# A hybrid mixer trunk: low weight parts behind high ones, additions moved off GpSimd, a new order of the first projections

## The chip, the cores and the metric

One core of a Trainium2 chip runs the whole program. The metric is device time in microseconds, from one launch; lower is better. Times before and after are medians of runs on a chip. TensorE, VectorE, ScalarE and GpSimd each execute their own list of instructions in order and wait for one another through semaphores; SyncE (SP) issues the DMAs.

## The reference

512 latent tokens and 256 context tokens of width 1024 go through two layers. In each layer all tokens are normalised, modulated and multiplied by one wide input matrix; three branches (gated DeltaNet, RG-LRU, neighbourhood attention) work on parts of the result; their outputs are gated, projected, merged and multiplied by an output matrix. The second layer yields latents alone.

```
h_lat = rms_norm(x, g_pre) * (1 + scale_l) + shift_l        # the same for context
p = h @ w_in        # split: DeltaNet q,k,v / gates / RG-LRU in / attention q,k,v / merge gates
q, k, v = silu(conv4(p[0]));  q, k = l2_normalize(q), l2_normalize(k)
q, k = axial_rope(q), axial_rope(k)                         # latents only
# DeltaNet, per chunk and direction, 4 heads:
u = w_v - w_k @ S;  o = (q*exp(gc)) @ S + (q k^T * decay) @ u
S = S * g_tail + (k * exp(gc[-1] - gc))^T @ u               # "key tail" times u
# merge
merged = sum_b sigmoid(gate_b) * (y_b @ w_branch[b]);  y = merged @ w_out
x = x + gate_l * rms_norm(y, g_post)
```

## The kernel before

**Arithmetic.** A float32 product is made of float16 matmuls: each weight block is split into a high part (`whi`, ScalarE) and a low part (`wlo`, VectorE: raw minus high), and the hidden state `h` likewise into two parts. `seg()` multiplies, for each of 8 (or 4) blocks of the contraction, high by high, high by low and low by high into one PSUM bank, 512 latent columns and then 256 context columns.

**Order by a planner.** The program's instruction lists are written by a planner, `Flow`. Python generators (tasks) issue instructions; `note()` assigns each VectorE, ScalarE and GpSimd instruction an estimated duration, and a task that yields a number sleeps that long in planned time. `fl.until(tile)` is the planned time until a tile is ready; `fl.fetched()` plans when a load lands. Tasks that are due run by rank; `main()` has the last rank, 9, and issues all projections, so a task with work ready puts its matmuls ahead of main()'s. A yield is no instruction and no wait on the chip: it only moves what other tasks issue meanwhile. `copy()` picks VectorE or ScalarE by which is planned to be sooner.

**Weights.** `schedule()` lists a layer's projections; `Weights` loads their blocks in that order through a ring of three raw buffers, splits them (`split()`; for attention and merge-gate weights, the names in `FINE`, in two parts of 4 blocks, each high part followed by its low part) and hands them out (`take()`).

**Around the layer.** `startup()` loads, normalises and modulates the tokens and computes the list's first three projections; at the end of a layer `layer()` does so for the next one, from `out_tail()`'s tiles. `out_tail()` takes one tile of 128 tokens through the output norm, the residual addition (first half of the columns on GpSimd, second on VectorE), the next layer's norm, eight transposes, the modulation (multiply on VectorE, addition on GpSimd) and the split into `h`.

**DeltaNet.** `gdn_front()` takes a projected tile (`a`) into a convolution buffer, of which there are two, shared with rotated queries; main() stands there until one is free. `gdn_prep()` convolves, transposes, rotates (products on VectorE, their sum on GpSimd) and normalises; one tile's preparation begins when the tile before has been read. `gdn_direction()` has one pass per direction over six chunks: `pre()` builds decay, key products (`lh`, `ll`) and the key tail `ktl` (GpSimd), `inverse()` the triangular inverse, `chain()` the recurrence.

**Modulation of the next layer.** `mod_rows()` is a side generator of main(): main() advances it with `next(side)` between merge-gate projections; it issues one load ahead and then four matmuls on the load before. It yields nothing that the planner reads.

Every VectorE, ScalarE and GpSimd instruction is recorded under line 195 (the `Engine` wrapper), matmuls under 258, transposes under 262, modulation matmuls under 467, so tiles' names tell them apart: `pl` are transposes in `gdn_prep`, `qt` and `kt` rotated queries and keys, `py` the output product, `xTp` the boundary's transposes, `pm` the modulation's product, `hx` the modulated tile, `lss` the squared norms, `pr` attention weights, `ld` a mask product of `lh`.

Of the kernel before, what the change touches and what calls it, by code (L numbers as in the profile page):

```python
# [17 lines left out]
P = 128  # L18
# [8 lines left out]
EPS = 1e-6  # L27
# [22 lines left out]
class Flow:  # L50
# [4 lines left out]
    def __init__(self):  # L55
        self.now, self.tasks = 0.0, []
        self.free, self.ready, self.used, self.near = {}, {}, {}, {}
        self.banks, self.kept, self.wire, self.ring = [None] * 5, set(), 0.0, []
        self.spent, self.touch, self.sp = set(), {}, 0.0
# [30 lines left out]
    def note(self, eng, op, args, kw):  # L90
        aps = [x for x in list(args) + list(kw.values()) if isinstance(x, bass.AP)]
        ins = aps[1:]
        n = max(math.prod(x.shape[1:]) for x in aps)
        start = max([self.free.get(eng, 0.0)] + [self.ready.get(x.name, 0.0)
                                                  - (LAT / 2 if self.near.get(x.name) == eng else 0.0) for x in ins])
        for x in ins:
            if x.space == PSUM and self.touch.get(x.name, (eng,))[0] != eng:
                start = max(start, self.touch[x.name][1] + LAT)
        if eng == "act":
            us = (n / 1200.0 + 0.09 + 0.09 * sum(isinstance(kw.get(x), bass.AP) for x in ("scale", "bias"))  # L100
                  + 0.2 * (kw.get("accum_out") is not None))
        elif op == "tensor_tensor_scan":
            us = n / 480.0 + 0.11
        elif eng == "pool":
            us = (n / 510.0 + 0.1 if n < 512 else n / 375.0) if op == "tensor_tensor" else n / 1000.0 + 0.12
        else:
            fast = (op == "tensor_scalar" and all(x.space == aps[0].space for x in ins)
                    or all(x.dtype == F16 for x in aps))
            us = n / (1920.0 if fast else 960.0) + 0.07 + 0.06 * sum(x.shape[1:] == (1,) for x in ins)
        end = self.free[eng] = start + us  # L110
        self.last = (start, us)
        for x in ins:
            self.used[x.name] = max(self.used.get(x.name, 0.0), end)
            if x.space == PSUM:
                self.touch[x.name] = (eng, end)
        for x in (aps[0], kw.get("accum_out")):
            if x is not None:
                self.ready[x.name] = end + LAT
                self.near[x.name] = eng
# [84 lines left out]
def schedule(l):  # L204
# [6 lines left out]
    s = [a0[0], a0[1], z[0], a0[2], z[1], a0[3], z[2], a0[4], z[3], a0[5]]  # L211
    s += kqv[0] + kqv[1] + kqv[2]
# [17 lines left out]
def build(tc, A, out):  # L230
# [88 lines left out]

    def rsqrt(dst, v, n, tag):  # L320
# [3 lines left out]
        V.tensor_scalar(yg[:, 0].bitcast(I32), v.bitcast(I32), -0.5, float(0x5F3759DF - (1 << 31)),  # L324
                        op0=OP.mult, op1=OP.add)
# [29 lines left out]
    class Weights:  # L355
# [19 lines left out]
        def split(self, pool_=None):  # L375
            if self.raw:
# [14 lines left out]
                for k in range(0, nk, step):  # L391
                    ks = slice(k, min(nk, k + step))
                    S.activation(hi[:, ks], raw[:, ks], AF.Copy, scale=SW)
                    yield fl.until(hi)
                    V.scalar_tensor_tensor(lo[:, ks], raw[:, ks], SW, hi[:, ks], op0=OP.mult, op1=OP.subtract)
# [3 lines left out]
        def take(self, key):  # L399
            yield lambda: self.pair and self.pair[0][3]  # L400
            hi, lo, k, _ = self.pair.pop(0)
            assert k == key, (k, key)
            return hi, lo
# [17 lines left out]
    def seg(dst, off, w, ks, nk, xs, a, b, ahead=False):  # L421

        hi, lo = w
        for k in ks:
            for n, (wt, part) in enumerate(((hi, 0), (hi, 1), (lo, 0))):
                mm(dst[:, a - off:b - off], wt[:, k, :], xs(part, k, a, b), start=(k == 0 and n == 0),
                   stop=(k == nk - 1 and n == 2))
                if n < 2:
                    yield 0.0
            if ahead and k == 0:  # L430
                W.ahead()
            yield 0.0
# [24 lines left out]
    def mod_rows(l, part, fin, load):  # L457
# [3 lines left out]
        yield  # L461
        pm = pst(f"pm{l}_{part}", [P, 512], keep=True)
        for k in range(KD):
# [8 lines left out]
            if k < KD - 1:  # L472
                nxt_ = load(l, part, k + 1)
                yield
# [72 lines left out]
    def tile_rstd(ss, dst, scale, tag):  # L547
        v = small.tile([P, 1], F32, tag=tag + "v", name=tag + "v")
        V.tensor_scalar(v, ss, scale, EPS, op0=OP.mult, op1=OP.add)
# [172 lines left out]
    def layer(l, mod, first):  # L722
# [345 lines left out]
        def gdn_prep(gp, which, hl, b, half, state, before):  # L1068
# [45 lines left out]
            yield fl.until(tmp)  # L1114
            G.tensor_tensor(dst[:, :LT, :], dst[:, :LT, :], tmp, OP.add)
            yield fl.until(ss)
            V.tensor_scalar(ss[:, :nt], ss[:, :nt], EPS, 128.0 if which == "q" else 1.0, op0=OP.add, op1=OP.mult)
# [72 lines left out]
        def gdn_direction(gp, half, d):  # L1190
# [15 lines left out]
            def pre():  # L1206
                yield ended(dcy, *preps[:4])
                for s in range(TT):
# [64 lines left out]
                    G.tensor_tensor(ktl, kt[:, :, t_, :], dec[:, :, edge:edge + 1].to_broadcast(HALF), OP.mult)  # L1273
# [206 lines left out]
        def out_tail(pp, t, py, xt, gg, h, nmod, before):  # L1480
# [12 lines left out]
            for hf in range(2):  # L1493
# [3 lines left out]
                (G, V)[hf].tensor_tensor(xo[:, cols], xo[:, cols], xt[:, cols], OP.add)  # L1497
# [14 lines left out]
            for q in range(2):  # L1512
# [6 lines left out]
                V.tensor_tensor(hx_, pt, nmod["sa"][:, ks, s:s + 1].to_broadcast([P, 4, P]), OP.mult)  # L1519
                yield fl.until(hx_)  # L1520
                G.tensor_tensor(hx_, hx_, nmod["sb"][:, ks, s:s + 1].to_broadcast([P, 4, P]), OP.add)
                yield fl.until(hx_)
# [32 lines left out]
        with ExitStack() as layer_:  # L1555
# [10 lines left out]
            opening = False  # L1566
            for tkn in schedule(l):
# [16 lines left out]
                if kind == "out":  # L1584
                    for _ in side:
                        pass
# [7 lines left out]
                if kind == "g":  # L1594
                    next(side, None)
# [51 lines left out]
                elif kind == "g":  # L1647
# [5 lines left out]
                    next(side, None)  # L1653
# [5 lines left out]
                    if m == KD - 1:  # L1659
                        for _ in side:  # L1660
                            pass
# [142 lines left out]
```

## Time and profile before

| what | value |
|---|---|
| median of 3 runs | 1758.42 us (1755.01 to 1759.4) |
| profiled execution, time / span | 1761.13 us / 1759.4 us |
| TensorE busy | 1647.0 us, 94%, 11452 matmuls |
| VectorE / ScalarE / GpSimd busy | 1190.2 / 858.1 / 350.6 us |
| granted TensorE clock, mean | 0.979 |
| DMA | 139.79 MB, mean 79 GB/s |

Busy time counts instructions that execute; a busy TensorE is not one at its peak. Idle time matters on the engine that the others wait for.

### The profile page before, as it was taken

Reading aid. Unit: us, or ns where it says so; the run is one execution under the profiler, and the core shown is the slowest. Engines: PE = TensorE matmul, PEld = TensorE weight load, DVE = VectorE, ACT = ScalarE, POOL = GpSimd, SP = SyncE. Lnnn points to the kernel's source line nnn. Section 1 sums busy time; section 2 is a strip of 40 time slices with the busy share of each in tenths; the row PEclk is TensorE's granted clock in tenths of the full one; section 3 lists DMA queues with packets and bytes.
Section 4 is the critical chain, followed back from the end, with each engine's and each line's share of the span. In section 5 each row is a group of like instructions: output and inputs, shape, how many; then the busy total and the mean of one; then the engine's idle time right before and its main releaser. Section 6 shows DMA issues by size and latency. Waiting matters only on the chain. (4 is left out here: it accounts for less than half of the span.)

```text
span 1759.4 us, 30281 instructions
## 1 busy us (share of the span) xinstructions
PE 1647.0 (94%) x11452; PEld 1030.7 (59%) x11452; DVE 1190.2 (68%) x2784; ACT 858.1 (49%) x2050; POOL 350.6 (20%) x506
## 2 busy tenths in 40 slices
PE   5979999999999999999999787999999999999998
PEld 3655878766677566455554444677755666533433
DVE  5566787766777458664536674988677886766643
ACT  5345666545555256542423233666455664665331
POOL 0104121002321002222212202431004320113211
PEclk9999999999999999999999888999999999999999
DMA  9111111121222421332422111111221113233522
GB/s 354 52 50 48 43 42 39 55 66 43 85 65 70 125 84 55 120 117 88 150 73 79 41 49 36 53 40 31 67 78 45 47 42 104 84 109 113 173 90 72
DMA packets 48386, 139.79 MB, mean 79 GB/s; under 512 B 8048, under 2 KB 8688, under 8 KB 48240
## 3 DMA queue, kind: packets, MB, share of 16 engines
q1 hardware_dynamic: 48240, 137.86, 24.4%
q8 instruction: 90, 1.47, 0.3%
q14 instruction: 56, 0.46, 0.1%
HBM read 133.64 MB, written 4.19 MB: 78 GB/s over the span
## 5 line engine op out<-in xcount | busy, mean ns | idle before, releaser
L258 PEld LDWEIGHTS <-whi_g 128*128 128x128 f16 x1152 | 109.9, 98 | 89.8 <-issue 10.3
L258 PE MATMUL 1_g<-h,whi_g 128*128 128x512 f16 x384 | 119.6, 387 | 4.4 <-ACT whi_g L195 4.4
L258 PE MATMUL 0_g<-h,whi_g 128*128 128x512 f16 x384 | 116.7, 380 | 0.0
L258 PE MATMUL py<-wo,mg 128*128 128x512 f16 x480 | 104.9, 379 | 0.0
L258 PEld LDWEIGHTS <-whi_a 128*128 128x128 f16 x704 | 70.3, 100 | 50.9 <-issue 10.1
L195 ACT ACTIVATE di<-py 64x128 f16<-64x128 f32 x255 | 68.5, 271 | 53.9 <-PE py L258 22.7
L195 DVE SCALAR_TENSOR_TENSOR wlo_g<-raw,whi_g 128x512 f16<-128x512 f32 x96 | 87.2, 933 | 7.0 <-ACT whi_g L195 7.0
L195 DVE SCALAR_TENSOR_TENSOR coa<-cba,cva,coa 128x770 f32<-128x770 f32 (+1 forms) x72 | 74.3, 1032 | 23.8 <-ACT coa L195 23.3
L258 PEld LDWEIGHTS <-wlo_g 128*128 128x128 f16 x576 | 56.7, 98 | 45.1 <-DVE wlo_g L195 5.0
L258 PEld LDWEIGHTS <-whi_b 128*128 128x128 f16 x576 | 54.7, 98 | 46.6 <-issue 7.0
L195 ACT ACTIVATE X<-px 128x256 f16<-128x256 f32 x164 | 60.8, 381 | 40.3 <-PE px L258 37.6
L258 PEld LDWEIGHTS <-mg 128*128 128x128 f16 x480 | 47.0, 98 | 55.1
L258 PE MATMUL 1_g<-h,wlo_g 128*128 128x512 f16 x192 | 74.5, 388 | 3.0 <-DVE wlo_g L195 3.0
L195 DVE SCALAR_TENSOR_TENSOR wlo_b<-raw,whi_b 128x512 f16<-128x512 f32 x48 | 39.6, 825 | 51.9 <-ACT whi_b L195 51.8
L258 PE MATMUL 0_g<-h,wlo_g 128*128 128x512 f16 x192 | 72.8, 379 | 0.0
L195 DVE TENSOR_TENSOR ic<-pp,lmc 128x128 f16<-128x128 f32 x240 | 65.3, 283 | 3.6 <-PE pp L258 0.7
L195 POOL TENSOR_SCALAR_AFFINE_SELECT dec<-dec 128x256 f32<-128x256 f32 x48 | 22.7, 480 | 223.4 <-ACT dec L195 214.4
L195 ACT ACTIVATE whi_g<-raw 128x512 f16<-128x512 f32 x96 | 56.8, 623 | 20.3 <-DMA raw<-in_w_in 20.2
L195 POOL TENSOR_TENSOR gm<-trir,gst 128x256 fp32r<-128x256 f32 x96 | 65.2, 704 | 0.0
L195 POOL TENSOR_TENSOR ix<-ix,zz 128x1536 f32<-128x1536 f32 x8 | 27.6, 3449 | 176.0 <-ACT zz L195 176.0
L258 PEld LDWEIGHTS <-di 128*128 128x128 f16 x480 | 41.5, 98 | 27.5 <-issue 4.0
L195 POOL TENSOR_TENSOR mt<-mg,mt 128x768 f32<-128x768 f32 (+1 forms) x16 | 30.9, 1932 | 133.2 <-DVE mt L195 133.2
(653 smaller groups left out, 4816.8 us busy)
## 6 DMA issues: line engine op xcount, KB each, us to landing
raw<-in_w_in SPq DMA_DIRECT2D x128, 512.0 KB, 3.6
wm<-in_w_mod SPq DMA_DIRECT2D x48, 512.0 KB, 3.7
raw<-in_w_branch SPq DMA_DIRECT2D x48, 256.0 KB, 2.6
rwo<-in_w_out SPq DMA_DIRECT2D x16, 512.0 KB, 3.5
xt<-in_xin SPq DMA_DIRECT2D x12, 512.0 KB, 4.9
bias<-in_rpb SPq DMA_DIRECT2D x24, 256.0 KB, 2.8
lw<-in_lru_w SPq DMA_DIRECT2D x8, 256.0 KB, 2.9
x<-xo SPq DMA_DIRECT2D x4, 512.0 KB, 2.9
```

The costliest lines, as they stand in the source:

```text
L195: return real(*args, **kw)
L258: nc.tensor.matmul(dst, lhsT, rhs, **kw)
```

## The change

Projections end with the low parts; high parts of a weight are all split before its low parts, and a projection waits, in planned time, for the high part at its start and for the low part ahead of the low products. Four kinds of GpSimd work move: the sum of the rotation, the key tail (now two VectorE scalings), half of the residual additions (VectorE), and the boundary's modulation, which becomes four ScalarE activations with scale and bias in place of one VectorE and one GpSimd instruction. The first list of a layer alternates DeltaNet and gate projections from the start. Side generators yield the tile they wait for, and main() sleeps until it is planned to have landed. The planner charges more for Identity activations and for VectorE instructions with two SBUF inputs that overlap GpSimd work, and some tiny `tensor_scalar` steps get another form with constant tiles. Cut to its core:

```diff
         self.banks, self.kept, self.wire, self.ring = [None] * 5, set(), 0.0, []
-        self.spent, self.touch, self.sp = set(), {}, 0.0
+        self.spent, self.touch, self.sp, self.pool = set(), {}, 0.0, []
...
             us = (n / 1200.0 + 0.09 + 0.09 * sum(isinstance(kw.get(x), bass.AP) for x in ("scale", "bias"))
-                  + 0.2 * (kw.get("accum_out") is not None))
+                  + 0.2 * (kw.get("accum_out") is not None) + 0.1 * (AF.Identity in args))
         elif op == "tensor_tensor_scan":
...
             us = n / (1920.0 if fast else 960.0) + 0.07 + 0.06 * sum(x.shape[1:] == (1,) for x in ins)
+        if eng == "dve" and sum(x.space != PSUM for x in ins if x.shape[1:] != (1,)) > 1:
+            us += 0.35 * any(a < start + us and b > start for a, b in self.pool)
         end = self.free[eng] = start + us
         self.last = (start, us)
+        if eng == "pool" and us > 0.25:
+            self.pool = self.pool[-20:] + [(start, end)]
         for x in ins:
...
     za = [("za", i) for i in range(NH)]
-    s = [a0[0], a0[1], z[0], a0[2], z[1], a0[3], z[2], a0[4], z[3], a0[5]]
-    s += kqv[0] + kqv[1] + kqv[2]
+    s = [a0[0], z[0], a0[1], z[1], a0[2], z[2], a0[3], z[3], a0[4], kqv[0][0], a0[5]]
+    s += kqv[0][1:] + kqv[1] + kqv[2]
     s += [a1[0], kqv[3][0], a1[1], kqv[3][1], a1[2], kqv[3][2], a1[3], za[0], a1[4], za[1], a1[5], ("merge",)]
...
+    def const_t(name, shape, v, dt=F32):
+        t = cons.tile(shape, dt, name=name)
+        V.memset(t, v)
+        return t
+
+    eps_t = const_t("eps", [P, 1], EPS)
+    magic = const_t("magic", [P, 1], float(0x5F3759DF - (1 << 31)))
+    unit = {"k": const_t("one", [P, 1], 1.0), "q": const_t("dim", [P, 1], 128.0)}
+
     def rsqrt(dst, v, n, tag):
...
         t = small.tile([P, n], F32, tag=tag + "t", name=tag + "t")
-        V.tensor_scalar(yg[:, 0].bitcast(I32), v.bitcast(I32), -0.5, float(0x5F3759DF - (1 << 31)),
-                        op0=OP.mult, op1=OP.add)
+        V.scalar_tensor_tensor(yg[:, 0].bitcast(I32), v.bitcast(I32), -0.5, magic.to_broadcast([P, n]),
+                               op0=OP.mult, op1=OP.add)
         V.scalar_tensor_tensor(yg[:, 1], v, 0.5, yg[:, 0], op0=OP.mult, op1=OP.mult)
...
                 step = 4 if key[1] in FINE else KD
-                for k in range(0, nk, step):
-                    ks = slice(k, min(nk, k + step))
+                parts = [slice(k, min(nk, k + step)) for k in range(0, nk, step)]
+                for ks in parts:
                     S.activation(hi[:, ks], raw[:, ks], AF.Copy, scale=SW)
-                    yield fl.until(hi)
+                yield fl.until(hi)
+                for ks in parts:
                     V.scalar_tensor_tensor(lo[:, ks], raw[:, ks], SW, hi[:, ks], op0=OP.mult, op1=OP.subtract)
...
             assert k == key, (k, key)
+            yield fl.until(hi)
             return hi, lo
...
         for k in ks:
-            for n, (wt, part) in enumerate(((hi, 0), (hi, 1), (lo, 0))):
-                mm(dst[:, a - off:b - off], wt[:, k, :], xs(part, k, a, b), start=(k == 0 and n == 0),
-                   stop=(k == nk - 1 and n == 2))
-                if n < 2:
-                    yield 0.0
+            for part in range(2):
+                mm(dst[:, a - off:b - off], hi[:, k, :], xs(part, k, a, b), start=(k == 0 and part == 0), stop=False)
+                yield 0.0
             if ahead and k == 0:
                 W.ahead()
+        yield fl.until(lo)
+        for k in ks:
+            mm(dst[:, a - off:b - off], lo[:, k, :], xs(0, k, a, b), start=False, stop=(k == nk - 1))
             yield 0.0
...
         nxt_ = load(l, part, 0)
-        yield
+        yield nxt_
         pm = pst(f"pm{l}_{part}", [P, 512], keep=True)
...
                 nxt_ = load(l, part, k + 1)
-                yield
+                yield nxt_
         yield from fin(pm)
...
         v = small.tile([P, 1], F32, tag=tag + "v", name=tag + "v")
-        V.tensor_scalar(v, ss, scale, EPS, op0=OP.mult, op1=OP.add)
+        V.scalar_tensor_tensor(v, ss, scale, eps_t, op0=OP.mult, op1=OP.add)
         rsqrt(dst, v, 1, tag)
...
                                 C["sin"][:, ts, :].rearrange(sw, two=2, q=32), OP.mult)
-            yield fl.until(tmp)
-            G.tensor_tensor(dst[:, :LT, :], dst[:, :LT, :], tmp, OP.add)
+            V.tensor_tensor(dst[:, :LT, :], dst[:, :LT, :], tmp, OP.add)
             yield fl.until(ss)
-            V.tensor_scalar(ss[:, :nt], ss[:, :nt], EPS, 128.0 if which == "q" else 1.0, op0=OP.add, op1=OP.mult)
+            V.scalar_tensor_tensor(ss[:, :nt], ss[:, :nt], EPS, unit[which].to_broadcast([P, nt]),
+                                   op0=OP.add, op1=OP.mult)
             rsqrt(r[:, :nt], ss[:, :nt], nt, f"l{nt}")
...
                     ktl = gtile("ktl", 2)
-                    G.tensor_tensor(ktl, kt[:, :, t_, :], dec[:, :, edge:edge + 1].to_broadcast(HALF), OP.mult)
+                    for u in range(2):
+                        V.tensor_scalar(ktl[:, u, :], kt[:, u, t_, :], dec[:, u, edge:edge + 1], None, op0=OP.mult)
                     bb = bst[:, s, d, hs].unsqueeze(2).to_broadcast(HALF)
...
                                        op0=OP.mult, op1=OP.mult)
-                (G, V)[hf].tensor_tensor(xo[:, cols], xo[:, cols], xt[:, cols], OP.add)
+                V.tensor_tensor(xo[:, cols], xo[:, cols], xt[:, cols], OP.add)
                 if last:
...
                 hx_ = pp.tile([P, 4, P], F32, tag="hx", name="hx", bufs=4)
-                V.tensor_tensor(hx_, pt, nmod["sa"][:, ks, s:s + 1].to_broadcast([P, 4, P]), OP.mult)
-                yield fl.until(hx_)
-                G.tensor_tensor(hx_, hx_, nmod["sb"][:, ks, s:s + 1].to_broadcast([P, 4, P]), OP.add)
-                yield fl.until(hx_)
+                for k in range(4):
+                    S.activation(hx_[:, k, :], pt[:, k, :], AF.Identity, scale=nmod["sa"][:, 4 * q + k, s:s + 1],
+                                 bias=nmod["sb"][:, 4 * q + k, s:s + 1])
                 S.activation(h[:, 0, ks, cols], hx_, AF.Copy)
...
             outs, qk, gates, sums = [], {}, {}, {}
-            opening = False
+            opening, need = False, None
             for tkn in schedule(l):
...
                 if kind == "out":
-                    for _ in side:
-                        pass
+                    for need in side:
+                        if need is not None:
+                            yield fl.until(need)
+                    need = None
                     yield core
...
                 if kind == "g":
-                    next(side, None)
+                    if need is not None:
+                        yield fl.until(need)
+                    need = next(side, None)
                 if kind == "xb" and tkn[1]:
...
```

## Rows read from the trace of the kernel before

**Rows 1.** The page: busy time of an engine, its share, instructions.

```profile
PE 1647.0 (94%) x11452; PEld 1030.7 (59%) x11452; DVE 1190.2 (68%) x2784; ACT 858.1 (49%) x2050; POOL 350.6 (20%) x506
```

**Rows 2.** Stretches: length; PE, PEld, DVE, ACT, POOL busy (instructions); PEclk, DMA share, GB/s.

```profile
360.00:400.00 40.00, 39.94 (x261) 27.75 (x260) 29.01 (x69) 20.94 (x55) 3.72 (x9) 1.00 0.19 59
...
1040.00:1080.00 40.00, 27.92 (x139) 14.82 (x137) 20.92 (x46) 17.35 (x50) 4.38 (x9) 0.87 0.08 27
...
1360.00:1400.00 40.00, 36.93 (x342) 25.77 (x340) 35.48 (x104) 25.54 (x79) 14.08 (x24) 1.00 0.20 61
1400.00:1440.00 40.00, 36.84 (x339) 25.88 (x338) 36.33 (x111) 24.25 (x73) 13.24 (x24) 1.00 0.13 41
```

**Rows 3.** TensorE's waits: what waits, for whom; us in total, times, longest us.

```profile
PE pl L262 <- DVE qt L195: 14.4, 2, 7.7
PE xTp L262 <- DVE sq L195: 9.7, 1, 9.7
PE pm L467 <- DMA wm<-in_w_mod: 8.5, 5, 2.7
...
PE 1_a_q L258 <- DVE wlo_a L195: 4.9, 1, 4.9
...
PE 1_a_v L258 <- DVE wlo_a L195: 4.4, 2, 2.5
...
PE 1_g L258 <- DVE wlo_g L195: 3.0, 3, 1.6
...
PE 0_a_q L258 <- DVE wlo_a L195: 1.9, 1, 1.9
...
PE 1_za L258 <- DVE wlo_za L195: 1.2, 1, 1.2
```

**Rows 4.** The chain of waits near 1693 us: start, duration, what.

```profile
1693.70 5.18 PE 1_g L258 x24
```

**Rows 5.** TensorE in order of time, 104 to 132 us; wait before in brackets.

```profile
109.61 0.63 PE L262 MATMUL pl<-ident,kt 128*128 128x128 f32 x4 [0.30 <-DVE kt L195]
...
118.00 0.27 PE L258 MATMUL 0_a_v_0c<-h,wlo_a 128*128 128x256 f16 x1
125.02 1.11 PE L262 MATMUL pl<-ident,qt 128*128 128x128 f32 x4 [6.75 <-DVE qt L195]
```

**Rows 6.** All engines in order of time, 118 to 127 us.

```profile
119.46 1.88 POOL L195 TENSOR_TENSOR qt<-qt,rope 128x512 f32<-128x512 f32 x1 [14.76 <-DVE rope L195]
120.14 1.23 DVE L195 TENSOR_SCALAR lss<-lss 128x6 f32<-128x6 f32 x1
```

**Rows 7.** All engines in order of time at the layer boundary.

```profile
977.09 0.68 DVE L195 TENSOR_TENSOR hx<-xTp,sa 128x512 f32<-128x512 f32 x1
...
979.78 1.49 POOL L195 TENSOR_TENSOR hx<-hx,sb 128x512 f32<-128x512 f32 x1
...
984.49 0.68 DVE L195 TENSOR_TENSOR hx<-xTp,sa 128x512 f32<-128x512 f32 x1
```

**Rows 8.** Groups by form: busy us, mean ns of one | idle before, releasers.

```profile
L195 POOL TENSOR_TENSOR ll<-gm,lh 128x256 f16<-128x256 f32 x48 | 37.7, 785 | 32.8 <-ACT lh L195 32.8
L195 POOL TENSOR_TENSOR ktl<-kt,dec 128x256 f32<-128x256 f32 x48 | 33.2, 691 | 0.0
...
L195 POOL TENSOR_TENSOR hx<-hx,sb 128x512 f32<-128x512 f32 x12 | 14.7, 1229 | 30.2 <-DVE hx L195 26.0 <-DVE nss L195 4.2
...
L195 DVE TENSOR_SCALAR lss<-lss 128x6 f32<-128x6 f32 x12 | 8.6, 715 | 0.0
```

**Rows 9.** By tile: instructions, ns shortest/median/longest, first and last start.

```profile
L195 DVE TENSOR_SCALAR pr<-pr,st x40: 335/486/1694, 202.1 to 1321.6; 128x512 f32<-128x512 f32 x32, 128x256 f32<-128x256 f32 x8
...
L195 ACT ACTIVATE oa<-pq,egc x34: 348/361/368, 215.0 to 1426.3; 128x128 f32<-128x128 f32 x34
...
L195 DVE TENSOR_TENSOR ld<-lh,bd x48: 277/384/761, 159.5 to 1445.8; 128x256 f16<-128x256 f16 x48
```

More of the change, by code (lines that the diff above doesn't have):

```diff
@@ L1652, in layer @@
                     fl.drop(*[p for p, _ in both(o)])
-                    next(side, None)
+                    if need is not None:
+                        yield fl.until(need)
+                    need = next(side, None)
                     y = (ya, yb, yc)[br]
@@ L1659, in layer @@
                     if m == KD - 1:
-                        for _ in side:
-                            pass
+                        for need in side:
+                            if need is not None:
+                                yield fl.until(need)
+                        need = None
             if not last:
```

## The prediction

> **What bounds the kernel now.** I read the engine shares first: TensorE is busy for 94% of the span, VectorE for 68% [rows 1]. Then the stretches: at 360 to 400 us TensorE is busy for 39.94 of 40 us, so there only less matmul work would help, and the change removes none. Elsewhere it is not: 27.92 of 40 at 1040, 36.93 and 36.84 at 1360 and 1400, where VectorE is nearly full with 35.48 and 36.33 [rows 2]. What can be won is TensorE's idle time, and the view of its waits names it [rows 3]: low weight parts that VectorE delivers late (4.9, 4.4, 1.9, 3.0 and 1.2 us, 15.4 in all), the transposes of a rotated query (14.4), the transposes at the layer boundary (9.7), modulation weights (8.5). The reader is to see that these are few, long stalls of an engine that issues in order, not a steady shortage of a resource. A second loss hangs on them: in the stretch with 27.92 us of work the granted clock is 0.87, a mixture of the 1.2 and 2.4 GHz levels [rows 2], and four transposes behind a 6.75 us gap take 1.11 us where the same four took 0.63 before it [rows 5].
>
> **The sum's base.** The profiled execution took 1761.1 us around a span of 1759.4; the median of the runs, 1758.4, is 2.7 us less. I add up against 1761.1 and take off 2.7 at the end.
>
> **A. Low parts last.** Now the first low product is the third matmul of a projection; after the change it is the seventeenth. 24 matmuls of 512 columns take 5.18 us [rows 4], 0.216 each, so the low part may come 14 x 0.216 = 3.0 us later. Of the single stalls in [rows 3] only the 4.9 is longer, and leaves 1.9: the gain is 15.4 - 1.9 = 13.5. For the fine-split weights the low part is also issued behind the second high half, a delay inside the 3.0. The 3.0 and 1.2 lie where VectorE is nearly full; I give half of them back, 2.1, and take 11. Bounds: 0, if VectorE's order slips as far as TensorE's, to 15.4. The number of matmuls and weight loads is unchanged.
>
> **B. Alternating projections.** At 118.27 us TensorE ends the first value projection, then has nothing until the rotated query's transposes at 125.02 [rows 5]. Only main() issues projections, and it stands in gdn_front() until one of two convolution buffers is free; the next one, the fourth z, is queued behind that. In the new list this z precedes the value projection. A projection over latents and, with half as many columns, context is 5.18 + 2.6 = 7.8 us [rows 4], longer than the gap, and the query's own chain starts no later, since it waits for the key before it and not for TensorE. So the 6.75 us gap is filled, and likewise the rest of the 14.4 in layer 1. The attention key moved between the two value projections supplies the 7.8 us that the z no longer does there. I take 12: 14.4 less a new wait of 1.2 for each layer, because the convolutions stay a chain of latencies. Bounds: -5 (the gap reappears behind the second value) to 14.4. The same loads are issued in SP's queue in another order, none added.
>
> **Clock.** Four transposes lose 1.11 - 0.63 = 0.5 us behind such a gap [rows 5], and the projection behind runs slow for some time still. For the five long gaps of A and B I estimate 1 us each: 5, bounds 0 to 10.
>
> **C. Layer boundary.** TensorE's 9.7 us wait is that of one tile's tail on an in-order VectorE: the modulation multiply of one half starts at 977.09, of the other at 984.49, with another tile's normalisation between; the GpSimd add on the first half takes 1.49 us, behind the residual add on the same engine [rows 7]. The change takes the 12 multiplies off VectorE and the 12 adds (1229 ns, [rows 8]) off GpSimd and puts 48 Identity activations on ScalarE. The trace has no such operation; the nearest row, a scaled copy of 128x128 from PSUM, is 361 ns [rows 9], so four are 1.4 us, against 0.68 + 1.23 = 1.9 us and one more hand-over. That is only 0.5 for each half-tile, but the second half no longer queues behind a foreign reciprocal root. The residual add costs VectorE about 0.68, the nearest duration [rows 7], in place of GpSimd's parallel work; behind the last tile the two additions then run one after the other without a partner, which I cost at 0 (between -0.7 and +0.7). I take 6 of the 9.7 for C; bounds 0 (the context tiles become the last) to 11.
>
> **D. Planner waits for modulation weights.** No instruction waits for more than before: only the list that the planner writes changes, so tasks that are ready get their matmuls ahead of the modulation's. Where no task is ready, the stall stays; and main()'s next gate projection, queued behind the wait, is held as it is now behind the stalled matmul. Of 8.5 us I take 3; bounds 8.5 and, where the planner thinks the load later than it is, -2. The loads keep their place on SP.
>
> **E. Work off GpSimd.** 48 key tails of 691 ns leave GpSimd [rows 8] and become 96 VectorE scalings of 128x128. The trace has scalings of SBUF tiles with 256 columns (at least 335 ns) and 512 (median 486) [rows 9]; along that line 128 columns are 335 - 75 = 260 ns, so 25 us. They are issued just behind GpSimd's ll (785 ns, [rows 8]). One row shows what happens then: a scaling of six columns lasts 1.23 us and ends with GpSimd's addition, 1.88 us from 119.46 [rows 6]. So up to 48 x 0.785 = 38 us more. Against that, ld, issued beside ll and the key tail, varies from 277 to 761 ns with a median of 384 [rows 9]; a return to 277 is 48 x 0.107 = 5 us back. The rotation sums add 16 x 0.68 = 11 us; the small scalings that now wait for them, 12 with a mean of 715 ns [rows 8], 8.6 us in all, give most of that back, I take 7. The constants and the changed form of the reciprocal-root steps I cost at nothing: tiny tiles either way. VectorE thus takes on 24 to 62 us over four head pairs. In layer 0 this lies beside a full TensorE [rows 2]; with that cover gone it would cost its 12 to 31. In layer 1, 12 to 31 us fall on stretches where VectorE has 4 of 40 us free; I charge 5. Bounds: 4 gained (a shorter GpSimd queue ahead of gm) to 50 lost.
>
> The Trainium skill, page "SBUF — State Buffer", section "Who interferes with whom", says that VectorE and GpSimd take one port pair as an exclusive lock, so a two-port operation blocks for a whole GpSimd instruction. The 1.23 us row agrees; by the rule every key tail that meets ll pays the full price, and the time would be that of the second rival below.
>
> **F. New stalls.** The planner's new costs (Identity, overlap with GpSimd) re-order every engine and move copies between ScalarE and VectorE, and another order draws other waits: I charge 6, a little less than one of the two 14.4/2 us stalls of today [rows 3]; bounds 0 and 15, both of them.
>
> **Sum.** 11 + 12 + 5 + 6 + 3 - 5 - 6 = 26 us. 1761.1 - 26 = 1735.1 in the profiled frame, 1732 as a median.
>
> **Rivals.**
> 1. The stalls only move. Work drawn forward to fill 118 to 125 us is missing later, and TensorE is held by the same convolution and inversion chains. For it: at 1040 us no engine is full [rows 2]. Against: at 360 us TensorE is full, so work done early shortens that stretch. A third of A, B and the clock (9) remains, less 5 for E: 1754.
> 2. VectorE becomes the bound in the DeltaNet chunks: slower. Place: the ranges at 1360 to 1440 and their like. Price: 25 for scalings, 38 for being blocked, 11 for rotation sums less 12 back, 62 in all, against gains of A to D and the clock of 37 less 6 for new stalls; the median is 1758.4 + 31 = 1789 if all of it lies on the path, and 1770 if 43 do. It decides once the added work exceeds the 3.7 to 4.5 free us of 40. For it: 36.33 of 40. Against: the two stretches shown have 8.2 us free, and a head pair, which lasts longer than these, adds 6 to 15.
> 3. All named stalls go: 15.4 + 14.4 + 9.7 + 8.5 with 8 of clock, 56 without E or F: 1702.
>
> **Chances and range.** My forecast 0.57, the first rival 0.17, the second 0.16, the third 0.10. A measurement of this kernel cannot tell changes under 0.3% (5.3 us) from none, so "same" is 1753.1 to 1763.7. The forecast and the third rival are faster, the first rival is faster for a third of its chance and otherwise same, the second slower but for a tenth: faster 0.73, same 0.12, slower 0.15. The range 1706 to 1762 holds the forecast, the first rival and most of the third; the slower rival is left outside with a little of the third. The forecast's own range is 1715 to 1750.
>
> **What would show it.** A: waits of TensorE on low parts under 5 us in all. B: no gap over 3 us ahead of the rotated query's transposes; instead the fourth z between second query and first value. C: boundary gap under 5 us. D: modulation waits near 5 us. E: key tails of about 260 ns, some up to 1 us, and VectorE above 36 of 40 us in layer 1's second head pair with TensorE no lower than 36.8. I am wrong if TensorE's idle time, 112 us now (1759.4 - 1647.0, [rows 1]), falls by less than 12, or if a new gap over 5 us appears in the convolution stage.

## The result and the profile after

The changed kernel takes 1718.7 us (median; runs from 1717.8 to 1720.4) beside 1758.4 for the kernel before: a ratio of 0.978 (95% interval 0.976 to 0.980), 39.8 us less. The forecast was 1732, its own range 1715 to 1750: the direction held, and so did the mechanism of its largest term, the low parts; the gain was half as large again as the 26 us of the sum.

The page of the changed kernel, first part, answers to [rows 1]:

```profile
span 1718.7 us, 30355 instructions
...
PE 1637.7 (95%) x11452; PEld 1027.7 (60%) x11452; DVE 1203.1 (70%) x2864; ACT 885.9 (52%) x2132; POOL 273.5 (16%) x420
```

TensorE issues the same 11452 matmuls. Its idle time falls from 112.4 to 1718.7 - 1637.7 = 81.0 us, and its busy time by 9.3 us, for the same work at a mean granted clock of 0.987 instead of 0.979. 31.4 and 9.3 are the whole 40.7 us between the two profiled spans.

The stretches of [rows 2], same columns, in the changed kernel (the same times hold somewhat later work in it):

```profile
360.00:400.00 40.00, 40.00 (x267) 28.49 (x266) 30.79 (x76) 21.60 (x57) 0.32 (x6) 1.00 0.19 60
1040.00:1080.00 40.00, 33.19 (x194) 20.47 (x193) 23.10 (x54) 17.93 (x46) 6.77 (x22) 0.91 0.17 53
1360.00:1400.00 40.00, 37.71 (x340) 26.56 (x340) 36.30 (x113) 24.50 (x74) 10.14 (x19) 1.00 0.18 54
1400.00:1440.00 40.00, 39.49 (x358) 27.03 (x357) 34.90 (x116) 27.20 (x83) 9.26 (x22) 1.00 0.16 48
```

At 1040 us TensorE does 33.19 us of work instead of 27.92, at a clock of 0.91 instead of 0.87. TensorE's waits, columns as in [rows 3]:

```profile
PE xTp L266 <- DVE xt L199: 16.7, 2, 12.7
PE pl L266 <- DVE qt L199: 8.1, 2, 5.4
PE xTp L266 <- DVE sq L199: 7.7, 1, 7.7
PE pm L483 <- DMA wm<-in_w_mod: 6.8, 4, 2.3
...
PE 1_z L262 <- DVE wlo_z L199: 1.6, 1, 1.6
```

The first of these is the load at the start, which the change leaves alone. Waits for low parts shrink from 15.4 us in [rows 3], 16.4 with those of `b` shown below, to 1.6, for rotated queries from 14.4 to 8.1, at the boundary from 9.7 to 7.7, for modulation weights from 8.5 to 6.8.

Where the time came from is best read in stages, cut at the same matmul in each profiled execution (us; "layer 0 in": to the first gate projection of layer 0; "layer 0 out": to its first output product; "boundary": to layer 1's last context projection; "layer 1 in": to its first gate projection; "DeltaNet 1": to its first RG-LRU projection, `1_xb`; "branches": to its last `1_zb`; "merge": to its last gate projection; "end"):

```
          layer0in layer0out boundary layer1in DeltaNet1 branches merge   end
before       428.5     480.1    105.0    330.5     142.5     60.3  159.8  52.8
after        426.3     474.5    101.5    315.5     139.1     60.3  148.9  52.6
gain           2.2       5.6      3.5     15.0       3.4      0.0   10.9   0.1
```

Layer 1's projections were expected to gain. The merge's 10.9 us were not: of the stalls that the forecast priced, only 1.5 us of A's low parts and 6.9 us of D's modulation weights lay there, and D was to win 3.

### The profile page after: what moved, and what is told of

Same layout as the page of the kernel before. It is cut to its first block, busy times and chain, and to the rows that moved or that the text cites. A ratio compares the mean times of both kernels' runs of the same rounds, so it can differ in the third digit from the quotient of the medians.

```text
span 1718.7 us, 30355 instructions
## 1 busy us (share of the span) xinstructions
PE 1637.7 (95%) x11452; PEld 1027.7 (60%) x11452; DVE 1203.1 (70%) x2864; ACT 885.9 (52%) x2132; POOL 273.5 (16%) x420
## 5 line engine op out<-in xcount | busy, mean ns | idle before, releaser
L199 DVE SCALAR_TENSOR_TENSOR wlo_g<-raw,whi_g 128x512 f16<-128x512 f32 x96 | 102.2, 1105 | 10.0 <-ACT whi_g L199 10.0
L199 ACT ACTIVATE X<-px 128x256 f16<-128x256 f32 x181 | 67.5, 381 | 56.4 <-PE px L262 50.9
L262 PE MATMUL 1_g<-h,whi_g 128*128 128x512 f16 x384 | 96.1, 386 | 0.0
L262 PE MATMUL 0_g<-h,whi_g 128*128 128x512 f16 x384 | 92.0, 379 | 0.0
L199 POOL MEMSET cba<- 128x2 f32 (+1 forms) x72 | 3.6, 98 | 495.3 <-DVE coa L199 235.8
L199 DVE CAST di<-py 64x128 f16<-64x128 f32 x127 | 36.5, 288 | 24.4 <-ACT di L199 20.3
L262 PE MATMUL pp<-X,ld 128*128 128x64 f16 x480 | 51.4, 192 | 2.3 <-ACT di L199 0.7
```

What stands on the lines that cost most here:

```text
L199: return real(*args, **kw)
L262: nc.tensor.matmul(dst, lhsT, rhs, **kw)
```

## Experiments

Ratios are to the kernel before, in brackets the 95% interval; "costs" and "gains" are against the changed kernel's median of 1718.7 us.

### One part undone

**Low parts in turn again** (all of A undone: order of matmuls, split of the loads, the planner's wait for the high part ahead of the low):

```diff
-                parts = [slice(k, min(nk, k + step)) for k in range(0, nk, step)]
-                for ks in parts:
+                for k in range(0, nk, step):
+                    ks = slice(k, min(nk, k + step))
...
-                yield fl.until(hi)
-                for ks in parts:
+                    yield fl.until(hi)
...
-            yield fl.until(hi)
...
-            for part in range(2):
-                mm(dst[:, a - off:b - off], hi[:, k, :], xs(part, k, a, b), start=(k == 0 and part == 0), stop=False)
...
+            for n, (wt, part) in enumerate(((hi, 0), (hi, 1), (lo, 0))):
+                mm(dst[:, a - off:b - off], wt[:, k, :], xs(part, k, a, b), start=(k == 0 and n == 0),
+                   stop=(k == nk - 1 and n == 2))
...
-        yield fl.until(lo)
-        for k in ks:
-            mm(dst[:, a - off:b - off], lo[:, k, :], xs(0, k, a, b), start=False, stop=(k == nk - 1))
```

> The changed kernel (1718.7 us) with the low parts back in their old place: third matmul of each block, each fine-split high part followed by its low part, no planned wait for the high part. Theory 1, low parts last are a gain by themselves (terms A and its clock, 11 to 16 us): 1730 to 1735, and TensorE's waits on low parts are back at 10 us or more (1.6 in the changed kernel). Theory 2, the gain came from the other parts and the low parts were waited for only because other work came late: within 5 us of 1718.7, waits on low parts under 6 us. Theory 3, the whole gain is a lucky order of the planner's list: any time between 1715 and 1760, without the waits on low parts accounting for the difference.

Measured: 1738.9 us, 0.989 (0.988 to 0.991): A is worth 20.2 us inside the change. TensorE waits of this kernel:

```profile
PE 1_g L262 <- DVE wlo_g L199: 3.6, 4, 1.7
...
PE 1_z L262 <- DVE wlo_z L199: 2.9, 1, 2.9
PE 1_g L262 <- ACT whi_g L199: 2.0, 1, 2.0
```

Only 8.5 us of waits on weight parts are in the list, so 20.2 us are more than the stalls that bear their name. 10.5 of them lie in the merge, which takes 159.4 us here. Layer 0's input stage is even 4.9 us shorter without A (421.4): A is no gain everywhere.

**Order of matmuls alone undone**, the last part of that diff without the first:

```diff
-            for part in range(2):
+            for n, (wt, part) in enumerate(((hi, 0), (hi, 1), (lo, 0))):
...
-        yield fl.until(lo)
-        for k in ks:
```

> The changed kernel with only the order of the matmuls back (each block's low product behind its two high ones); high parts are still split first and a projection still waits, in planned time, for its high part. Undoing all three cost 20 us. Theory 1, TensorE's slack of fourteen matmuls is the gain: 1734 to 1740, and the stage of merge gates from the last zb to the last gate of layer 1 is back near 159 us (148.9 in the changed kernel). Theory 2, the planned waits and the split order are the gain: under 1724, the stage under 152.

Measured: 1749.4 us, 0.994 (0.993 to 0.995). By the ratios this costs 28 us, outside both theories and more than undoing all of A (20). So the gain hangs on the order of the matmuls, and beside the old order the split and the planner's wait do harm; the new order without these two was not run. The merge takes 157.0 us. Waits for weight parts are back:

```profile
PE 1_g L262 <- DVE wlo_g L199: 6.6, 6, 2.3
...
PE 1_g L262 <- ACT whi_g L199: 3.7, 2, 2.1
```

**Old list of projections** (B undone):

```diff
-    s = [a0[0], z[0], a0[1], z[1], a0[2], z[2], a0[3], z[3], a0[4], kqv[0][0], a0[5]]
-    s += kqv[0][1:] + kqv[1] + kqv[2]
+    s = [a0[0], a0[1], z[0], a0[2], z[1], a0[3], z[2], a0[4], z[3], a0[5]]
+    s += kqv[0] + kqv[1] + kqv[2]
```

> The changed kernel with the old list of first projections. Theory 1, alternation fills the two gaps ahead of the rotated query (term B with its clock, 12 to 15 us): 1731 to 1734, and the waits of pl for qt, 8.1 us in the changed kernel, are back at 14 us. Theory 2, the gap is bound by the convolution chain and the order only moves it: within 4 us of 1718.7 with the milestone 'first merge gate of layer 0' (426.3 us) unchanged within 2 us.

Measured: 1735.6 us, 0.988 (0.986 to 0.990): 17.0 us. The waits for the rotated query are back to what [rows 3] had:

```profile
PE pl L266 <- DVE qt L199: 14.9, 2, 8.1
...
PE pl L266 <- DVE coa L199: 3.2, 1, 3.2
```

**Boundary back on VectorE and GpSimd** (C undone):

```diff
-                    S.activation(hx_[:, k, :], pt[:, k, :], AF.Identity, scale=nmod["sa"][...], bias=nmod["sb"][...])
+                V.tensor_tensor(hx_, pt, nmod["sa"][...].to_broadcast([P, 4, P]), OP.mult)
...
+                G.tensor_tensor(hx_, hx_, nmod["sb"][...].to_broadcast([P, 4, P]), OP.add)
...
-                V.tensor_tensor(xo[:, cols], xo[:, cols], xt[:, cols], OP.add)
+                (G, V)[hf].tensor_tensor(xo[:, cols], xo[:, cols], xt[:, cols], OP.add)
```

> The changed kernel with the boundary's modulation back on VectorE and GpSimd and half of the residual additions back on GpSimd. Theory 1 (term C): the boundary gap ahead of xTp, 7.7 us in the changed kernel, grows to 10 or more, and the whole to 1722 to 1726, the difference arising between 900 and 1010 us. Theory 2, the boundary is one tile's chain whose length the four activations (456 ns each) do not shorten: within 3 us of 1718.7.

Measured: 1722.7 us, 0.980 (0.978 to 0.981), which overlaps the changed kernel's interval. The place itself is plain: the boundary stage takes 106.7 us instead of 101.5, and its gap is the old one again:

```profile
PE xTp L266 <- DVE sq L199: 9.8, 1, 9.8
```

**Planner's wait for modulation weights taken out** (D undone):

```diff
-        yield nxt_
+        yield
```

> The changed kernel with side generators that yield nothing, so main() advances them without waiting for a planned landing. Theory 1 (term D): 1720 to 1724, with the waits of pm at 8 us or more (6.8 in the changed kernel). Theory 2, no task is ready where the loads are late, so the order hardly changes: within 2 us of 1718.7 and the waits of pm within 1 us of 6.8.

Measured: 1724.3 us, 0.981 (0.979 to 0.982): overlapping again, so its worth, from nothing to some 10 us, stays open. Settled is that it does not shorten the stall that it is aimed at. TensorE waits no longer for modulation weights than with the planner's wait (6.8):

```profile
PE pm L483 <- DMA wm<-in_w_mod: 6.5, 4, 2.2
```

**Key tail back on GpSimd** (E, its larger half, undone):

```diff
-                    for u in range(2):
-                        V.tensor_scalar(ktl[:, u, :], kt[:, u, t_, :], dec[:, u, edge:edge + 1], None, op0=OP.mult)
+                    G.tensor_tensor(ktl, kt[:, :, t_, :], dec[:, :, edge:edge + 1].to_broadcast(HALF), OP.mult)
```

> The changed kernel with the key tail back on GpSimd as one 128x256 product. Theory 1 (term E): the move cost about 5 us, so this is faster, 1711 to 1717. Theory 2, the key tail on GpSimd was what slowed two-input VectorE work beside it and GpSimd's own queue (ld median 384 ns before, 284 after): slower, 1720 to 1728, with ld's median back near 380 ns.

Measured: 1710.1 us, 0.973 (0.971 to 0.975), clear of the changed kernel's interval: without this edit the change is 8.5 us faster.

**Rotation sum and the small scalings back on GpSimd** (E, the rest):

```diff
-            V.tensor_tensor(dst[:, :LT, :], dst[:, :LT, :], tmp, OP.add)
+            G.tensor_tensor(dst[:, :LT, :], dst[:, :LT, :], tmp, OP.add)
...
```

> The changed kernel with the rotation's sum back on GpSimd and the small scaling behind it a tensor_scalar again. Theory 1: the sums shorten the chain of each rotated tile by about half a microsecond to one, 16 tiles, of which two hold TensorE up: 1720 to 1722, waits of pl for qt up by 1 to 3 us from 8.1. Theory 2, VectorE's additional 11 us cost as much as the chain gains: within 2 us of 1718.7. Theory 3, like the key tail it is better on GpSimd: 1712 to 1716.

Measured: 1718.1 us, 0.977 (0.975 to 0.979): no difference. The wait for the rotated query does grow by the 1 to 3 us that the first theory named, from 8.1, without the whole growing:

```profile
PE pl L266 <- DVE qt L199: 10.3, 3, 5.8
```

**Old costs in the planner** (Identity and the overlap with GpSimd left out of its model):

```diff
-                  + 0.2 * (kw.get("accum_out") is not None) + 0.1 * (AF.Identity in args))
+                  + 0.2 * (kw.get("accum_out") is not None))
...
-        if eng == "dve" and sum(x.space != PSUM for x in ins if x.shape[1:] != (1,)) > 1:
-            us += 0.35 * any(a < start + us and b > start for a, b in self.pool)
```

> The changed kernel with the planner's old costs (nothing added for Identity or for VectorE work that overlaps GpSimd); every instruction is the same, only the order and the engine of copies may differ. Theory 1 (term F): such a re-ordering is worth a few microseconds either way, 1712 to 1726, and no single stage accounts for it. Theory 2, the overlap cost is what took VectorE's two-input work from beside GpSimd's (ld median 284 ns, 384 before): slower by 4 or more, ld's median back over 350 ns.

Measured: 1716.7 us, 0.977 (0.975 to 0.979): no difference as a whole, and ld's median stays at 286 ns, against the second theory. But single stages do differ: the boundary takes 97.5 us instead of 101.5, and its gap ahead of the transposes is gone. The longest waits left in that stage are

```profile
PE f0c L260 <- ACT h L197: 2.2, 2, 1.8
```

DeltaNet 1 is 2.6 us shorter and the merge 1.9; layer 1's input stage is 2.3 us longer, layer 0's output stage 1.0.

### Parts alone on the kernel before

**A alone**, and **A with the new list**:

The first takes over A's part of the change (the reverse of the first diff here) and nothing else, the second also the new list:

```diff
-    s = [a0[0], a0[1], z[0], a0[2], z[1], a0[3], z[2], a0[4], z[3], a0[5]]
-    s += kqv[0] + kqv[1] + kqv[2]
+    s = [a0[0], z[0], a0[1], z[1], a0[2], z[2], a0[3], z[3], a0[4], kqv[0][0], a0[5]]
+    s += kqv[0][1:] + kqv[1] + kqv[2]
```

> The kernel before with the low parts last and nothing else. Undone in the changed kernel it cost 20 us. If the parts add up, 1758.4 - 20 = 1738 here (1734 to 1742). If low parts last pays only once the other stalls are gone, 1745 to 1752; my term A with its clock alone would give 1742 to 1747. The stage from the last zb projection to the last merge gate of layer 1, 159.8 us before and 148.9 changed, should be near 149 if low parts last is what shortens it.

> The kernel before with low parts last and the new list of first projections, nothing else. If those two add up (25.8 us alone and 17.0 undone): 1715 (1712 to 1720), so that all the other edits together are worth nothing. If they share gains, 1721 to 1728, and the other edits are worth the rest.

Measured: 1732.5 us, 0.985 (0.983 to 0.988), and 1730.6 us, 0.983 (0.982 to 0.984). A alone gains 25.8 us. Its page gives the two halves of that:

```profile
PE 1635.3 (94%) x11452; PEld 1029.5 (59%) x11452; DVE 1202.5 (69%) x2795; ACT 853.8 (49%) x2039; POOL 354.1 (20%) x506
```

In a span of 1732.2 us TensorE idles for 96.9, 15.5 less than before, and is busy for 11.7 us less with the same matmuls. B on top gains 1.8 at the medians, with overlapping intervals, though the same B is worth 17.0 once the other edits stand beside it. The merge shows A's unforeseen half. Columns as in [rows 2]; the kernel before, then the changed one, then A alone:

```profile
1546.80:1706.70 159.90, 146.13 (x650) 61.56 (x648) 99.75 (x123) 79.36 (x120) 36.52 (x21) 0.97 0.41 133
```

```profile
1517.20:1666.10 148.90, 143.57 (x650) 61.65 (x648) 106.73 (x123) 79.34 (x119) 38.55 (x21) 0.98 0.45 143
```

```profile
1529.70:1679.80 150.10, 140.57 (x649) 61.00 (x648) 107.12 (x123) 79.18 (x119) 37.08 (x21) 1.00 0.45 142
```

The same matmuls (one record is missing) take 9.8 us less with A alone: idle falls from 13.8 to 9.5, busy from 146.1 to 140.6 at a clock of 1.00 instead of 0.97. What idled there before, in the kernel before's waits of that stretch:

```profile
PE pm L467 <- DMA wm<-in_w_mod: 6.9, 4, 2.7
PE 1_g L258 <- ACT whi_g L195: 4.4, 2, 2.2
PE 1_g L258 <- DVE wlo_g L195: 1.5, 2, 0.7
PE b L258 <- DVE wlo_b L195: 1.0, 2, 0.6
```

In the changed kernel only the first of these is left, with 5.2; with A alone there is also one of 1.4 for a high part of `b`. So most waits for the high part, which ScalarE makes, went too.

### Other ways

**Key tail on ScalarE**, as two copies with a scale:

```diff
-                        V.tensor_scalar(ktl[:, u, :], kt[:, u, t_, :], dec[:, u, edge:edge + 1], None, op0=OP.mult)
+                        S.activation(ktl[:, u, :], kt[:, u, t_, :], AF.Copy, scale=dec[:, u, edge:edge + 1])
```

> The changed kernel with the key tail on ScalarE, two scaled copies of 128x128, in place of two VectorE scalings. With the key tail on GpSimd it took 1710.1. Theory 1, the 28 us of scalings on VectorE (96 of about 290 ns) are what costs: off VectorE by any way is a gain, 1709 to 1714. Theory 2, ScalarE, which feeds TensorE with X, Y and di in the same chunks, is no better a place: 1717 to 1727.

Measured: 1710.6 us, 0.973 (0.971 to 0.974): as good as on GpSimd. That two ways off VectorE give the same total speaks for the load on VectorE as what costs; the stages, under E below, do not show it. The tile on VectorE (changed kernel), on GpSimd and on ScalarE (count, ns shortest/median/longest, first and last start):

```profile
L199 DVE TENSOR_SCALAR ktl<-kt,dec x96: 269/282/733, 159.6 to 1420.8; 128x128 f32<-128x128 f32 x96
```

```profile
L199 POOL TENSOR_TENSOR ktl<-kt,dec x48: 610/620/1331, 160.3 to 1417.9; 128x256 f32<-128x256 f32 x48
```

```profile
L199 ACT ACTIVATE ktl<-kt,dec x96: 385/390/419, 159.0 to 1415.0; 128x128 f32<-128x128 f32 x96
```

**All that seemed useless undone at once** (the three diffs above of key tail, rotation sum and costs together):

> The changed kernel with the three edits undone that cost time or gave none alone: key tail and rotation sum back on GpSimd, old planner costs. If their single effects (-8.5, -0.6, -2.0 us) add up, 1707.5; if a re-ordering of the list is worth 5 us either way, 1703 to 1716; over 1718 would mean that the overlap cost is needed once GpSimd has its work back.

Measured: 1718.3 us, 0.977 (0.975 to 0.978). The single medians add up to 1707.5 (-8.5, -0.6 and -2.0); what came is 11 us more, at the edge of the last theory (over 1718), with runs from 1717.7 to 1722.5. So with the key tail on GpSimd nothing is gained in this order. The best versions that ran are the key tail on GpSimd (1710.1) and on ScalarE (1710.6).

## Why the prediction was right, and where it was off

**A. Low parts last: right, mis-sized.** Predicted 11, measured 25.8 alone and 20.2 inside the change. The sum took only the waits whose releaser was a low part and gave some of them back. Two things were left out: waits for the high part, 4.4 us in the merge; and most of the clock. Of the 27.2 us between the two profiled spans, A alone takes 15.5 off TensorE's idle time and 11.7 off its busy time, more than twice the 5 us of clock forecast for A and B together. In the merge 5.5 of the 9.8 us are the same matmuls at 1.00 instead of 0.97. That is hardly chance of one profile: the eleven kernels with the new order of matmuls are busy there for 140.2 to 143.6 us, the three with the old order for 144.5 to 147.2. The half of 3.0 and 1.2 that was given back for a full VectorE was not lost; half of the 3.0 lay in the merge, where VectorE is busy for 99.75 of 159.90 us. The slip allowed (3.0 us, 14 matmuls) proved ample, although the low parts became slower, 1105 ns instead of 933 on average:

```profile
L199 DVE SCALAR_TENSOR_TENSOR wlo_g<-raw,whi_g 128x512 f16<-128x512 f32 x96 | 102.2, 1105 | 10.0 <-ACT whi_g L199 10.0
```

Two of them, in order of time on the changed kernel, beside two operations of GpSimd and with no wait of TensorE behind (the first takes 3.58 us of the 5.26, so the low products at 1559.19, which start before its end, use a weight that was split earlier):

```profile
1555.36 3.44 POOL L199 TENSOR_TENSOR ix<-ix,zz 128x1536 f32<-128x1536 f32 x1 [13.22 <-ACT zz L199]
1555.72 3.14 PEld L262 LDWEIGHTS <-whi_g 128*128 128x128 f16 x16 [0.84 <-issue]
1555.72 3.63 PE L262 MATMUL 1_g<-h,whi_g 128*128 128x512 f16 x16
1555.77 5.26 DVE L199 SCALAR_TENSOR_TENSOR wlo_g<-raw,whi_g 128x512 f16<-128x512 f32 x2 [1.13 <-ACT whi_g L199]
...
1558.76 1.72 POOL L199 TENSOR_TENSOR mg<-mg,mt 128x512 f32<-128x512 f32 x1
...
1559.19 1.89 PE L262 MATMUL 1_g<-h,wlo_g 128*128 128x512 f16 x8
```

**B. Alternation: near in size inside the change (12 predicted, 17.0), half right in mechanism.** The fourth z does run between the second query and the first value projection (from 104.7 us). TensorE at the rotated query, changed kernel, layer 0 and layer 1:

```profile
121.83 1.04 PE L262 MATMUL 0_a_v_0c<-h,wlo_a 128*128 128x256 f16 x8
125.58 0.66 PE L266 MATMUL pl<-ident,qt 128*128 128x128 f32 x4 [2.71 <-DVE qt L199]
...
1053.59 1.11 PE L266 MATMUL pl<-ident,qt 128*128 128x128 f32 x4 [5.40 <-DVE qt L199]
```

The gap of [rows 5] shrank from 6.75 to 2.71, but layer 1's is still 5.40 where under 3 was forecast. The first rival shows too. At 320 us, the kernel before and the changed one:

```profile
320.00:360.00 40.00, 39.86 (x260) 27.30 (x259) 26.42 (x60) 20.77 (x56) 1.37 (x4) 1.00 0.18 54
```

```profile
320.00:360.00 40.00, 36.89 (x238) 23.35 (x235) 25.88 (x58) 20.73 (x61) 0.16 (x3) 1.00 0.12 41
```

TensorE lacks 3.0 us of work there that it had before; layer 0's input stage gained only 2.2 us. Undone, B costs 5.6 us in that stage (431.9) and 7.9 in layer 1's (323.4). That A with B gained no more than A alone was not foreseen, and which of the other edits B needs was not tried.

**Clock: right in kind, 5 predicted.** TensorE's busy time fell by 9.3 us for the same instructions, and by 11.7 with A alone. The rows above show how: behind the gap that shrank to 2.71 us, four transposes take 0.66 us, behind the one of 5.40 us 1.11. In the measured worths it is part of A and B.

**C. Boundary: right in sign, wrong in its chain.** Predicted 6 with a gap under 5 us; the stage gained 3.5 and the gap is 7.7. Four Identities take 1.50 us against 1.4 estimated (456 ns each at the median). But they were not what the gap was made of. The changed kernel, all engines, in order of time:

```profile
964.92 0.69 DVE L199 TENSOR_TENSOR xo<-xo,xt 128x512 f32<-128x512 f32 x1
...
966.15 1.50 ACT L199 ACTIVATE hx<-xTp,sb,sa 128x128 f32<-128x128 f32 x4 [6.11 <-PE xTp L266]
967.69 0.63 ACT L199 ACTIVATE h<-hx 128x512 f16<-128x512 f32 x1
968.22 0.58 ACT L199 ACTIVATE jk<-py 128x512 f16<-128x512 f32 x1
...
969.50 0.63 ACT L199 ACTIVATE jk<-xo 128x512 f16<-128x512 f32 x1
969.50 0.16 DVE L199 TENSOR_TENSOR nss<-nss 128x1 f32<-128x1 f32 x1 [0.46 <-ACT jk L199]
...
971.33 0.15 DVE L199 TENSOR_TENSOR nss<-nss 128x1 f32<-128x1 f32 x1
...
973.34 0.75 DVE L199 TENSOR_SCALAR sq<-xo,nr 128x1024 f32<-128x1024 f32 x1
...
974.24 1.09 PE L266 MATMUL xTp<-ident,sq 128*128 128x128 f32 x4 [7.68 <-DVE sq L199]
```

The tile's residual sum xo ends at 965.6, its squares start on ScalarE only at 969.50, behind the modulation (1.50), h and another tile's squares. Then two rounds of one-column steps on VectorE, from 969.50 and 971.33, lie ahead of sq. The prediction had looked at the modulation's own chain; the gap is the normalisation's, as the wait for sq in [rows 3] said, and the 1.50 us of hx now lie ahead of its squares. Still the move is a gain: undone, the gap is 9.8 us and the stage 5.2 us longer. And the 7.7 us that are left are a matter of order: with the planner's old costs, hx on ScalarE as here, the gap is gone and the stage takes 97.5 us, 7.5 less than before (96.6 in the run with three parts undone, which has the old costs too). It is term F's new costs, not the length of the chain, that kept C from its 6.

**D. Modulation weights: wrong.** Predicted 3. The waits fell to 6.8, but they are 6.5 without the planner's wait too. Which edit shortened them is open (6.8 also with the old list, 8.0 with A undone).

**E. Work off GpSimd: right in sign, too small, and not where it was charged.** Predicted -5; the key tail alone is -8.5. The scalings lasted 282 ns at the median (260 predicted) and 427 on average, so of the 38 us of blocking allowed some 96 x (0.427 - 0.269) = 15 came:

```profile
L199 DVE TENSOR_SCALAR ktl<-kt,dec 128x128 f32<-128x128 f32 x96 | 37.0, 427 | 0.0
```

By their times in the trace, 58 of them overlap a GpSimd operation and take 526 ns on average; the other 38 take 277. None paid for a whole ll: the longest is 464 ns above the shortest, and the shortest ll takes 662 ns.

The forecast charged nothing in layer 0 and 5 us in layer 1. With the tail on GpSimd 5.7 us come back in the four stages that have key tails, 3.8 in layer 0's (2.6 and 1.2) and 1.9 in layer 1's (0.4 and 1.5). Another 3.2 come in the merge, which has none. There TensorE idles for 5.3 us with either kernel and waits for modulation weights for 5.2; what differs is how long the same matmuls take, 140.38 us instead of 143.57, at a clock of 1.00 instead of 0.98:

```profile
1512.20:1657.90 145.70, 140.38 (x650) 61.08 (x648) 107.05 (x123) 79.35 (x119) 38.68 (x21) 1.00 0.46 146
```

Why the clock differs stays open. With the tail on ScalarE the 8.4 us between the profiled spans lie elsewhere: 3.7 in the merge and 1.2 at the boundary, neither of which has key tails, and layer 0's output stage is 1.1 us longer. So the totals agree and the places do not. That the load on VectorE costs is likely from the long scalings, but it is not shown; the rival, another order of the list with each variant, is not excluded, and with three parts undone at once the tail off VectorE gains nothing.

The second rival's mechanism is real at this size, not at its 62 us: VectorE stands at 36.30 and 34.90 of 40, as before, while TensorE does 3.4 us more in the same two stretches. The return of ld to 277 came (284 ns at the median), but ld is at 286 with the key tail on GpSimd, and at 287 with A alone, where nothing left GpSimd: it was not the moved work that had slowed it.

**F. New stalls: too dark.** 6 charged. No new gap over 5 us appeared in the convolution stages; the 5.40 is the rest of an old one (7.66). With the planner's old costs the whole is the same within noise, though by stages they do act, at the boundary above all. Neither sign of a wrong forecast came: idle time fell by 31 us, not by less than 12.

**Sum.** The parts undone cost 20.2 + 17.0 + 4.0 + 5.6 - 8.5 - 0.6 - 2.0 = 35.7 of the 39.8 us. That is near, but the kernel with three parts undone at once missed its own sum by 11 us and B's worth changed from 1.8 to 17.0, so single terms under some 10 us are not a property of an edit here. The step that was mis-sized is A with its clock: 11 us of stalls and a share of 5 us of clock were forecast, 15.5 us of idle time and 11.7 us of busy time came.

## What to carry to other kernels

Where one operand of an accumulation is late, issue the products that need it last: the order within the sum is free, and the slack it buys (14 matmuls here) took TensorE's waits for low parts from 16.4 us to 1.6. Waits for high parts went with them; by what part of the edit was not tried. Price a stall on TensorE with all waits of its kind and with the slow matmuls behind it, stage by stage, also in stages that the edit does not aim at. Before moving work off an idle engine, try each edit singly and then together: one edit here cost 8.5 us in a change that gained 39.8, and undone with two others it gained nothing.

## What was not expected of the hardware

- Scaling with a scale and a bias for each partition, 128x128 from PSUM on ScalarE: 456 ns; a copy of 128x128 with a scale alone took 390 from SBUF and 361 from PSUM [rows 9].
- VectorE's small operations beside GpSimd's are longer by no fixed share: the key tails range from 269 to 733 ns with a median near the shortest, while two low parts beside GpSimd operations of 3.44 and 1.72 us took 5.26 us together; the 49 low parts of the gates that meet no GpSimd operation take 681 ns on average.
